# A hybrid decoder layer in fp32: FFN and per-layer gate as Strassen products, the FFN's state in DRAM, the input projection in two kinds of passes, attention dealt out over the passes

## The chip, the core and the metric

The kernel runs on one NeuronCore of a Trainium2 chip. Its five engines run their own instruction streams and wait for each other by semaphores: TensorE (PE; its weight loads are listed apart as PEld), VectorE (DVE), ScalarE (ACT), GpSimd (POOL) and SyncE (SP), which here issues every DMA. The metric is the device time of one execution, in microseconds (us).

## The reference

One layer of a decoder trunk; 2048 tokens, model width 1024, everything fp32.

```python
u = rmsnorm(h, attn_pre_norm); proj = u @ w_in                  # 1024 -> 3584 columns
hq, hf, hi, hg, sq, sk, sv = split(proj)                        # 7 pieces of 512 columns
o_hg = rmsnorm(hgrn2_mix(hq, hf, hi, lb), hg_out_norm) * silu(hg)   # gated recurrence, 4 heads of 128x128 state
o_sb = rmsnorm(stick_breaking_mix(sq, sk, sv), sb_out_norm)         # 8 heads of width 64, strictly causal
h = h + rmsnorm(concat(o_hg, o_sb) @ w_out, attn_post_norm)
u = rmsnorm(h, ffn_pre_norm)
gate, up = split(u @ w_gate_up)                                 # 1024 -> 2 x 2816
y = (silu(gate) * up) @ w_down                                  # 2816 -> 1024
h = h + rmsnorm(y, ffn_post_norm)
out = h + (p @ ple_proj) * sigmoid(h @ ple_gate)                # p: 256 wide; gate 1024 -> 1024
```

Stick-breaking attention weighs key s for query t by sigmoid(z_ts) times the product of (1 - sigmoid(z_tj)) over the keys j between them: a running product along the keys, from the query backwards.

## The kernel before

The 2048 tokens are four groups of 512 (`GT`), g = 0 to 3. Every dense product is made of tiles of 128 x 128 (held in the array) by 128 x 512 (streamed), and each is computed three times for precision: an fp32 operand is split into a high part that the array takes and the remainder (`split`, L185-L189: ACT copies the high part, POOL or DVE subtracts), and `mm3` (L200-L203) adds high x high, high x low and low x high in a PSUM bank. Of a weight tile (`wr` raw, `wh` high, `wl` low; 128 x 512, loaded by SP, four raw buffers) ACT makes `wh` (L187) and POOL makes `wl` (L188). `dense` (L208) takes one weight tile after the other and issues four `mm3`, that is 12 matmuls of 512 columns, for each.

There are 3584 such `mm3`: 896 in the input projection, 256 in the output projection, 1408 in the gate and up half of the FFN, 704 in its down half, 256 in the per-layer gate and 64 in the projection of p.

The order of the work on PE is written out by hand: generators yield in small steps, and `weave` deals the steps of side streams evenly over the slots of a main stream. All other engines get their order from a scheduler that takes each instruction when its inputs should be ready, earlier program text first.

The side streams are attention and HGRN2. An attention unit is 128 queries by up to 512 keys of one head: PE makes `z` (L351), ACT the two sigmoids `f` and `be` (L359, L361), DVE the running product `pt` (a scan, L365) and the weights `a` = be x pt (L367); four units later PE transposes `a` into bank `tr` (L378), ACT and DVE split it into `ah` and `al` (L381, L383), PE multiplies by the values (`av`, L394-L395). There are 320 units: 32, 64, 96 and 128 for the four groups. HGRN2 runs in 45 steps a group: PE products in bank `hg`, masks and products on DVE (`score` L460, `ks` L480, `pd` L482) and on POOL (`qp` L478).

The stages follow each other like this. For each g, all seven pieces of the input projection of g (56 slots), with the attention units whose keys are ready and HGRN2 of g-1 between them. Then for g = 0 output projection and FFN, with the rest of attention (late units of groups 2 and 3) and HGRN2 of group 3 between them, up to the end of the FFN of group 0. Then for g = 1, 2, 3 output projection, per-layer gate of g-1 and FFN of g, with nothing beside them. The FFN of a group keeps its state (u, hidden tiles, y, h) in SBUF: eleven blocks of 256 gate and 256 up columns, the down product behind every second or third of them, then `post_y` (L686 and L542: norm, gain, residual).

## Time and profile before

| | us |
|---|---|
| runs of the kernel before, median of three | 3211.95 (3210.49 to 3213.1) |
| profiled execution, first to last instruction (span) | 3207.7 |
| PE busy in it | 3124.3 (97%) |
| DVE busy | 1774.9 (55%) |
| ACT busy | 1431.9 (45%) |
| POOL busy | 1494.0 (47%) |
| mean granted TensorE clock | 0.994 |

The span is 4.2 us under the median; that lies around the first and the last instruction. A row of a view names line, engine, operation and tiles (out<-in, `wl<-wr,wh`), shape and count. "Busy" of PE counts a matmul from its start to its modelled end, so PE can be shown busy while it loses a little. The views by window give, for a stretch of the span, its length, then busy time and instruction count of PE, PEld, DVE, ACT and POOL, then the granted clock, the busy share of the DMA engines and GB/s.

### The profile page before, as it was taken

Reading aid. Unit: us, or ns where it says so; the run is one execution under the profiler, and the core shown is the slowest. Engines: PE = TensorE matmul, PEld = TensorE weight load, DVE = VectorE, ACT = ScalarE, POOL = GpSimd, SP = SyncE. Lnnn points to the kernel's source line nnn. Section 1 sums busy time; section 2 is a strip of 40 time slices with the busy share of each in tenths; the row PEclk is TensorE's granted clock in tenths of the full one; section 3 lists DMA queues with packets and bytes.
Section 4 is the critical chain, followed back from the end, with each engine's and each line's share of the span. In section 5 each row is a group of like instructions: output and inputs, shape, how many; then the busy total and the mean of one; then the engine's idle time right before and its main releaser. Section 6 shows DMA issues by size and latency. Waiting matters only on the chain.

```text
span 3207.7 us, 44851 instructions
## 1 busy us (share of the span) xinstructions
PE 3124.3 (97%) x15328; PEld 2555.3 (80%) x15328; DVE 1774.9 (55%) x2492; ACT 1431.9 (45%) x2608; POOL 1494.0 (47%) x1254
## 2 busy tenths in 40 slices
PE   8999999999999799999999999999999998999999
PEld 6878878888888678888887888887888887888877
DVE  3356889888888888888866221226222226222142
ACT  4454565555456555555555332334333334332233
POOL 5444434443445423343346444556444556444453
PEclk9999999999999899999999999999999999999999
DMA  7666455545545233333343433332433333333333
GB/s 199 196 178 207 145 173 162 162 144 148 168 138 183 74 93 114 99 113 97 102 134 101 145 96 95 109 112 93 148 98 96 118 106 92 99 94 95 94 107 103
DMA packets 308420, 403.56 MB, mean 126 GB/s; under 512 B 35808, under 2 KB 177120, under 8 KB 308192
## 3 DMA queue, kind: packets, MB, share of 16 engines
q1 hardware_dynamic: 308192, 400.70, 41.1%
q8 instruction: 121, 1.98, 0.3%
q14 instruction: 107, 0.88, 0.1%
HBM read 341.85 MB, written 58.72 MB: 125 GB/s over the span
## 4 chain that ended last, share of the span: by engine, by line
PE 73%; DVE 6%; POOL 3%; issue 2%; ACT 1%; DMA 1%; SPq 0%; DVEq 0%; POOLq 0%; ACTq 0%
PE mm L201 16%; PE mm L203 15%; PE mm L202 15%; PE z L351 3%; PE tr L378 3%; PE av L201 2%; PE z L203 2%; PE z L201 2%; PE av L203 2%; PE av L202 2%; PE z L202 2%; DVE pt L365 2%; PE hg L449 2%; PE av L395 2%; POOL wl L188 1%
## 5 line engine op out<-in xcount | busy, mean ns | idle before, releaser
L188 POOL TENSOR_TENSOR wl<-wr,wh 128x512 fp32r<-128x512 f32 x896 | 1198.7, 1339 | 1415.0 <-ACT wh L187 1239.5
L187 ACT CAST wh<-wr 128x512 fp32r<-128x512 f32 x896 | 555.1, 620 | 1252.4 <-PE mm L202 422.5
L201 PE MATMUL mm<-uh,wh 128*128 128x512 f32 x1696 | 694.5, 410 | 5.3 <-DVE ea L321 4.6
L203 PE MATMUL mm<-uh,wl 128*128 128x512 f32 x1696 | 668.9, 394 | 1.0 <-POOL wl L188 0.9
L202 PE MATMUL mm<-ul,wh 128*128 128x512 f32 x1696 | 665.7, 393 | 0.0
L203 PEld LDWEIGHTS mm<-uh,wl 128*128 128x128 f32 x1696 | 318.6, 188 | 75.6 <-POOL wl L188 2.3
L201 PEld LDWEIGHTS mm<-uh,wh 128*128 128x128 f32 x1696 | 320.2, 189 | 68.9 <-DVE ea L321 5.6
L202 PEld LDWEIGHTS mm<-ul,wh 128*128 128x128 f32 x1696 | 320.3, 189 | 59.8
L365 DVE TENSOR_TENSOR_SCAN pt<-f,cy 128x513 f32<-128x513 f32 x192 | 294.5, 1534 | 69.1 <-ACT f L359 68.1
L645 DVE TENSOR_TENSOR tmp<-mm,tmp 128x512 f32<-128x512 f32 x67 | 45.4, 688 | 428.8 <-ACT tmp L644 428.6
L367 DVE TENSOR_TENSOR a<-be,pt 128x512 f32<-128x512 f32 (+2 forms) x320 | 256.7, 802 | 27.8 <-ACT ah L381 0.5
L381 ACT CAST ah<-tr 128x512 fp32r<-128x512 f32 (+1 forms) x320 | 167.1, 522 | 212.9 <-PE tr L378 209.7
L201 PE MATMUL mm<-wh,uh 128*128 128x512 f32 x616 | 255.0, 414 | 0.3 <-DVE ea L308 0.3
L202 PE MATMUL mm<-wl,uh 128*128 128x512 f32 x616 | 242.3, 393 | 8.0 <-POOL wl L188 8.0
L203 PE MATMUL mm<-wh,ul 128*128 128x512 f32 x616 | 243.0, 394 | 0.0
L365 DVE TENSOR_TENSOR_SCAN pt<-f 128x129 f32<-128x129 f32 (+3 forms) x128 | 163.4, 1277 | 124.6 <-ACT f L359 124.5
L383 DVE TENSOR_TENSOR al<-tr,ah 128x512 fp32r<-128x512 f32 (+1 forms) x320 | 192.4, 601 | 44.1 <-ACT ah L381 43.2
L359 ACT ACTIVATE f<-z 128x512 f32<-128x512 f32 (+2 forms) x320 | 170.0, 531 | 98.9 <-PE z L351 58.9
L201 PE MATMUL mm<-wh,hdh 128*128 128x512 f32 x520 | 209.0, 402 | 0.3 <-DVE tok L664 0.2
L203 PE MATMUL mm<-wh,hdl 128*128 128x512 f32 x520 | 205.3, 395 | 0.0
L202 PE MATMUL mm<-wl,hdh 128*128 128x512 f32 x520 | 205.0, 394 | 0.0
L351 PE MATMUL z<-kt,q 128*128 128x512 f32 (+3 forms) x640 | 183.7, 369 | 0.0
(252 smaller groups left out, 5157.2 us busy)
## 6 DMA issues: line engine op xcount, KB each, us to landing
wr<-in_w_gate_up_dram SPq DMA_DIRECT2D x704, 128.0 KB, 2.2
wr<-in_w_in_dram SPq DMA_DIRECT2D x224, 256.0 KB, 3.0
wr<-in_w_down_dram SPq DMA_DIRECT2D x176, 256.0 KB, 2.6
kt<-k_s SPq DMA_DIRECT2D x80, 256.0 KB, 3.0
vt<-v_s SPq DMA_DIRECT2D x80, 256.0 KB, 3.0
q<-q_s SPq DMA_DIRECT2D x128, 128.0 KB, 3.5
wr<-in_w_out_dram SPq DMA_DIRECT2D x64, 256.0 KB, 2.7
wr<-in_ple_gate_dram SPq DMA_DIRECT2D x64, 256.0 KB, 2.6
```

The lines of the kernel that those rows point to most:

```text
L187: nc.scalar.copy(hi, src)
L188: (lo_engine or nc.gpsimd).tensor_tensor(lo, src, hi.bitcast(F32), op=ALU.subtract)
L201: nc.tensor.matmul(o, l[0], r[0], start=start, stop=False)
L202: nc.tensor.matmul(o, l[0], r[1], start=False, stop=False)
L203: nc.tensor.matmul(o, l[1], r[0], start=False, stop=stop)
L351: nc.tensor.matmul(z[:, :n], st["q"][i][:, tb * P:(tb + 1) * P], ch["k"][:, :n], start=i == 0, stop=i == 1 and not diag)
L359: nc.scalar.activation(f[:, o:GT], z[:, :n], AF.Sigmoid, scale=-0.125)
L365: nc.vector.tensor_tensor_scan(pt[:, o:][:, ::-1], fr, fr, init, op0=ALU.mult, op1=ALU.bypass)
L367: nc.vector.tensor_tensor(a[:, :n], be[:, :n], pt[:, o + 1:], op=ALU.mult)
L378: nc.tensor.transpose(tr[:, tb * P:(tb + 1) * P], ch["a"][tb][:, sb * P:(sb + 1) * P], ident)
L381: nc.scalar.copy(hi[:, lo_c:], tr[:, lo_c:])
L383: nc.vector.tensor_tensor(lo[:, lo_c:], tr[:, lo_c:], hi[:, lo_c:].bitcast(F32), op=ALU.subtract)
```

## The change

**Products.** The gate/up product, the down product and the per-layer gate now work on two groups (1024 tokens) at a time and use one level of Strassen's scheme in Winograd's form: seven half-size block products in place of eight, with sums and differences of blocks before and behind them. The count of `mm3` falls from 1408 to 1232, from 704 to 616 and from 256 to 224; the other 1216 stay. The sums of weight blocks are made for each 256 columns anew on DVE (gate/up, per-layer gate) or POOL (down). The sums of `u` blocks (`t_set`) and of `h` blocks (`s_set`) are made once per pair of groups, those of the hidden tiles on POOL when they are produced. The results are combined by `chain` from PSUM on DVE, the down product keeps 28 tiles `y` and combines them in `post_y`, all on DVE and POOL.

**State in DRAM.** `u`, the residual `h` and `h2`, the transposed `u` and `h2`, the transposed p and seven hidden tiles per block go to DRAM scratch and come back by DMA.

**Prepared steps.** `drive` issues, for step n of a list of stages, first the loads, sums and splits (`prepare`) of step n+3 (gate/up, down) or n+1 (per-layer gate), then PE's products and `chain` of step n (`run`). All raw tiles come from ten `wr` buffers.

**Passes.** The input projection is cut into pass "a" (k, q, v: 24 slots) and pass "b" (the four HGRN2 pieces: 32 slots), in the order a0, a1, b0, a2, b1, a3, b2, b3. `plan` gives each pass its attention units and HGRN2 steps. The rest, 68 units, and HGRN2 of group 3 run with the output projections of groups 0, 1 and half of 2. The output projection of group 3 is put on PE behind the second step of the first gate/up stage. Attention is over when that stage begins.

**`a` on POOL.** The product be x pt moves from DVE to POOL.

```diff
-            nc.vector.tensor_tensor(a[:, :n], be[:, :n], pt[:, o + 1:], op=ALU.mult)
+            nc.gpsimd.tensor_tensor(a[:, :n], be[:, :n], pt[:, o + 1:], op=ALU.mult)
...
+    plan = [
+        ("a", 1, units[0], 0), ("b", 0, units[1] // 2, 0),
+        ("a", 2, units[1] - units[1] // 2, 19), ("b", 1, 44, 26),
+        ("a", 3, 32, 19), ("b", 2, 40, 26), ("b", 3, 40, 38),
+    ]
...
+    rates = Rate(att_stream, 2, todo, 2 * OP_SLOTS + OP_SLOTS // 2)
...
+    def t_set(blk, out, prod):
+        nk = ND // 2
+        if prod in (1, 2):
+            out[prod] = [pair_of(load(blk(prod - 1, 0, k)), "u", prod, G) for k in range(nk)]
+        elif prod == 6:
...
+        elif prod == 3:
+            out[3], out[5], out[4] = [], [], []
+            for k in range(nk):
+                b22, b21 = load(blk(1, 1, k)), load(blk(1, 0, k))
+                out[3].append(pair_of(b22, "u", 3, G))
+                sub(V, b21, b22, b21)
+                b12, b11 = load(blk(0, 1, k)), load(blk(0, 0, k))
+                sub(V, b12, b12, b11)
+                out[5].append(pair_of(b12, "u", 5, V))
+                sub(V, b21, b21, b12)
+                out[4].append(pair_of(b21, "u", 4, G))
...
+    def gate_up(grp):
...
+            def prepare(prod):
...
+                elif prod == 6:
+                    w, a21, a22 = wload(0, 0), wload(1, 0), wload(1, 1)
+                    s["s1"] = [acc("s1") for _ in range(2)]
+                    for n in range(2):
+                        add(V, s["s1"][n], a21[n], a22[n])
+                        sub(V, w[n], s["s1"][n], w[n])
...
+                s[prod] = [pair_of(t, "w", prod, G) for t in w]
+                if fb == 0:
+                    t_set(ublk, tt, prod)
+            def run(prod):
+                for q in range(2):
+                    b = mm_bank()
+                    for k in range(ND // 2):
+                        o = (k % 2) * 256 + q * P
+                        mm3(b, [t[:, o:o + P] for t in s[prod][k // 2]], tt[prod][k], k == 0, k == ND // 2 - 1)
+                    chain(prod, cs[q], b)
...
+    def down(grp):
...
+            def prepare(prod):
+                hs = [pair_in(hid_s[grp][f0 + k, prod - 1], prod, V) for k in range(nk)]
...
+                s[prod] = (hs, [pair_of(t, "w", prod, G) for t in w])
+            def run(prod):
...
+                    else:
+                        add(V, accs[i][prod], b, accs[i][prod])
+                if f0 + nk == nfb and prod == DOWN[-1]:
+                    for i in range(TT):
+                        post_y(grp, i, accs[i])
+    def post_y(grp, i, y):
+        add(G, y[2], y[1], y[2])
...
+        for half, halves in enumerate(((y[2], y[3]), (y[4], y[5]))):
+            r = row_rstd(halves)
+            for j, t in enumerate(halves):
+                gy = load(ffn_post_norm[0:1][:, cs].to_broadcast((P, GT)))
+                nc.vector.scalar_tensor_tensor(t, t, r, gy, op0=ALU.mult, op1=ALU.mult)
+                hr = load(h_s[g][i * P:(i + 1) * P, cs])
+                add(V, t, t, hr)
+                nc.sync.dma_start(h2_s[g][i * P:(i + 1) * P, cs], t)
+    def drive(stages, hooks):
+        steps = [(a, st, i, n) for a, (st, n) in enumerate(stages) for i in range(len(st))]
+        done = 0
+        for at, (a, st, i, n) in enumerate(steps):
+            while done < len(steps) and done <= at + steps[done][3]:
+                _, st2, i2, _ = steps[done]
+                st2[i2][0]()
+                done += 1
+            st[i][1]()
...
+    stages = [(gate_up(0), 3), (down(0), 3), (gate_up(1), 3), (down(1), 3), (ple(0), 1), (ple(1), 1)]
+    stages[0][0][2] = (lambda: (start_last(), third[0]()), third[1])
```

Three places show how the order moves.

POOL beside the output projection with attention. Before, beside the FFN of group 0 with attention and HGRN2 of group 3 (`qp` is HGRN2's, `wl` the split of a weight tile):

```order
L478 TENSOR_TENSOR qp<-qp,pd 128x64x4
L188 TENSOR_TENSOR wl<-wr,wh 128x512 x3
L478 TENSOR_TENSOR qp<-qp,pd 128x32x8
L188 TENSOR_TENSOR wl<-wr,wh 128x512 x3
L478 TENSOR_TENSOR qp<-qp,pd 128x16x16
```

Now (output projection of group 1), where `a` is the attention weight of a unit:

```order
L388 TENSOR_TENSOR a<-be,pt 128x512
L499 TENSOR_TENSOR qp<-qp,pd 128x32x8
L207 TENSOR_TENSOR wl<-wr,wh 128x512
L388 TENSOR_TENSOR a<-be,pt 128x512
L499 TENSOR_TENSOR qp<-qp,pd 128x16x16
L388 TENSOR_TENSOR a<-be,pt 128x512
L207 TENSOR_TENSOR wl<-wr,wh 128x512
L388 TENSOR_TENSOR a<-be,pt 128x512
```

Between two weight splits there stand now one or two `a`, which wait for DVE's scan.

DVE at the end of the down product. Before, `post_y` of a group is twelve instructions (four of them 1024 wide), and behind it come the splits of the transposed tiles and the next output projection:

```order
L666 TENSOR_TENSOR tok<-mm,tok 128x512 x3
L542 SCALAR_TENSOR_TENSOR tok<-tok,rstd_22280,tmp 128x512 x2
L542 SCALAR_TENSOR_TENSOR tok<-tok,rstd_22287,tmp 128x512 x2
L686 TENSOR_TENSOR h<-h,tok 128x1024 x2
L542 SCALAR_TENSOR_TENSOR tok<-tok,rstd_22294,tmp 128x512 x2
L686 TENSOR_TENSOR h<-h,tok 128x1024
```

Now, behind the first down stage, the tail of `post_y` stands ahead of the last sums of `u` blocks (`wr<-wr`), which the fourth step of the second gate/up stage needs:

```order
L954 SCALAR_TENSOR_TENSOR y<-y,rstd_24161,wr 128x512
L725 TENSOR_TENSOR y<-y,wr 128x512
L954 SCALAR_TENSOR_TENSOR y<-y,rstd_24184,wr 128x512
L725 TENSOR_TENSOR y<-y,wr 128x512
L954 SCALAR_TENSOR_TENSOR y<-y,rstd_24184,wr 128x512
L725 TENSOR_TENSOR y<-y,wr 128x512
L722 TENSOR_TENSOR wr<-wr 128x512 x5
L709 TENSOR_TENSOR ul<-wr,uh 128x512
L722 TENSOR_TENSOR wr<-wr 128x512 x3
L709 TENSOR_TENSOR ul<-wr,uh 128x512
```

From the last result of the down product to the first two of these sums there are 61 DVE instructions.

DVE where a per-layer gate begins. Before (group 0), it takes the gate's results from PSUM, adds the residual, and splits the next group's transposed tiles:

```order
L714 TENSOR_TENSOR tok<-mm,tok 128x512
L715 TENSOR_TENSOR tok<-tok,h 128x512
L714 TENSOR_TENSOR tok<-mm,tok 128x512
L714 TENSOR_TENSOR tok<-z,tok 128x512
L715 TENSOR_TENSOR tok<-tok,h 128x512
L251 SCALAR_TENSOR_TENSOR ul<-tr,g_ffn,uh 128x512
```

Now the splits of the second step (`ul<-wr,uh` x4) stand behind all of `post_y`, and the sums and splits of the third step behind those:

```order
L725 TENSOR_TENSOR y<-y,wr 128x512
L709 TENSOR_TENSOR ul<-wr,uh 128x512 x4
L725 TENSOR_TENSOR wr<-wr 128x512
L725 TENSOR_TENSOR c_30873<-tr,cu 128x512
L722 TENSOR_TENSOR wr<-wr 128x512 x3
L725 TENSOR_TENSOR wr<-wr 128x512
L709 TENSOR_TENSOR ul<-wr,uh 128x512
L725 TENSOR_TENSOR c_30888<-mm,cu 128x512
```

The last result of the down product stands 46 instructions ahead of the end of those four splits, and the last split of the third step 35 further on.

748 lines of the change are left out of this document (488 added, 260 removed).

## The prediction

> **What bounds the kernel now.** I read the page's busy times and its chain first, then windows, then the rows of the instructions that the change multiplies.
>
> ```profile
> span 3207.7 us, 44851 instructions
> PE 3124.3 (97%) x15328; PEld 2555.3 (80%) x15328; DVE 1774.9 (55%) x2492; ACT 1431.9 (45%) x2608; POOL 1494.0 (47%) x1254
> PE 73%; DVE 6%; POOL 3%; issue 2%; ACT 1%; DMA 1%; SPq 0%; DVEq 0%; POOLq 0%; ACTq 0%
> ```
>
> PE is busy for 3124 of 3208 us and carries the chain: the kernel is PE-bound, and 83 us are all the idle time that a better order alone could win. The windows (length, then busy time and count of PE, PEld, DVE, ACT, POOL, then clock, DMA share, GB/s) show where the 83 lie and what a matmul costs:
>
> ```profile
> 0.00:80.00 80.00, 65.86 (x290) 53.34 (x291) 24.50 (x44) 34.85 (x60) 40.57 (x61) 1.00 0.71 199
> 480.00:560.00 80.00, 77.22 (x449) 64.18 (x448) 72.69 (x112) 42.17 (x83) 32.68 (x29) 1.00 0.60 164
> 1080.00:1120.00 40.00, 23.11 (x107) 17.19 (x108) 38.24 (x65) 22.34 (x43) 20.09 (x22) 0.70 0.13 37
> 1680.00:1760.00 80.00, 74.32 (x342) 59.19 (x340) 53.30 (x58) 42.16 (x74) 55.40 (x50) 1.00 0.34 107
> 1840.00:1920.00 80.00, 80.00 (x345) 64.39 (x344) 18.26 (x26) 24.69 (x41) 36.93 (x29) 1.00 0.31 93
> 2160.00:2240.00 80.00, 77.19 (x359) 62.42 (x358) 48.62 (x55) 36.54 (x63) 50.26 (x46) 1.00 0.30 95
> 2640.00:2720.00 80.00, 74.01 (x344) 59.45 (x342) 50.00 (x54) 38.52 (x67) 52.74 (x49) 1.00 0.30 93
> ```
>
> From 1840 to 1920 PE does nothing but FFN products: 345 matmuls in 80 us, 0.232 us each, with DVE busy for 18 and POOL for 37 us. From 480 to 560, with attention beside the input projection, DVE is busy for 72.7 of 80. At 1080 to 1120 PE stands for 17 us at clock 0.70: the chain there runs through the norm between output projection and FFN of group 0.
>
> ```profile
> 1091.40 5.39 POOL rstd L224
> 1099.33 1.21 DVE h L614
> ```
>
> **What is removed on PE.** The products fall from 3584 to 3288 `mm3`: 296 x 3 = 888 matmuls fewer, transposes unchanged. 888 x 0.232 = 206 us. PE's busy time becomes 3124 - 206 = 2918 us. This is counted; the question is what the other engines give back.
>
> Old idle time that goes with the old stage boundaries: 17 us at 1080 to 1120 (the output projections of groups 1 and 2 now stand between this norm and its reader), 6 at 1680, 3 at 2160 and 6 at 2640: together 32, and some 3 us of the slow clock, so 35. The 14 us of the start stay.
>
> **What is added on DVE and POOL.** Rows of single instructions, ns min/median/max, and mean behind the bar:
>
> ```profile
> L365 DVE TENSOR_TENSOR_SCAN pt<-f,cy x192: 1265/1299/2409, 336.3 to 1644.7; 128x513 f32<-128x513 f32 x192
> L367 DVE TENSOR_TENSOR a<-be,pt x320: 279/692/1821, 100.2 to 1646.1; 128x512 f32<-128x512 f32 x96, 128x128 f32<-128x128 f32 x32, 128x384 f32<-128x384 f32 x32
> L188 POOL TENSOR_TENSOR wl<-wr,wh x896: 1260/1292/2463, 17.4 to 3193.8; 128x512 fp32r<-128x512 f32 x180
> L188 DVE TENSOR_TENSOR hdl<-tmp,hdh x88: 669/679/1794, 1176.5 to 3080.5; 128x512 fp32r<-128x512 f32 x88
> L542 DVE SCALAR_TENSOR_TENSOR tok<-tok,rstd,tmp x64: 716/747/1784, 1082.0 to 3122.9; 128x512 f32<-128x512 f32 x64
> L383 DVE TENSOR_TENSOR al<-tr,ah 128x512 fp32r<-128x512 f32 x224 | 152.7, 682 | 30.1 <-ACT ah L381 29.3
> L478 POOL TENSOR_TENSOR qp<-qp,pd 128x256 f32<-128x256 f32 x112 | 96.9, 865 | 185.8 <-PE hg L449 102.0 <-issue 33.0 <-PE hg L456 17.2
> L480 DVE TENSOR_TENSOR ks<-ks,pd 128x256 f32<-128x256 f32 x112 | 62.4, 557 | 2.2 <-PE hg L456 2.1
> ```
>
> A 512-wide step is 1.26 to 1.29 us on POOL and 0.67 to 0.69 on DVE. But DVE instructions whose inputs are both in SBUF (L365, L367, L188, L542) reach 1.8 to 2.4 us, while `al`, which reads PSUM, has a mean of 682 ns, as good as its best. The timeline shows why, in three pairs (start us, us):
>
> ```profile
> 405.03 1.93 DVE L365 TENSOR_TENSOR_SCAN pt<-f 128x513 f32<-128x513 f32 x1 [1.98 <-ACT f L359]
> 404.58 1.29 POOL L188 TENSOR_TENSOR wl<-wr,wh 128x512 fp32r<-128x512 f32 x1 [3.67 <-ACT wh L187]
> 338.03 1.82 DVE L367 TENSOR_TENSOR a<-be,pt 128x512 f32<-128x512 f32 x1
> 338.01 1.29 POOL L188 TENSOR_TENSOR wl<-wr,wh 128x512 fp32r<-128x512 f32 x1 [1.17 <-ACT wh L187]
> 378.73 1.26 DVE L365 TENSOR_TENSOR_SCAN pt<-f,cy 128x513 f32<-128x513 f32 x1
> 379.07 2.02 POOL L188 TENSOR_TENSOR wl<-wr,wh 128x512 fp32r<-128x512 f32 x1 [1.06 <-ACT wh L187]
> ```
>
> They take turns. The scan ends 1.09 us after POOL's end (405.87), DVE's product 0.55 after it (339.30), and in the last pair POOL ends 1.10 after the scan (379.99). So a turn costs 1.09 us for a scan, 0.55 for a DVE step, 1.10 for a POOL step: about 0.2 us of each lie under the other's turn. I go by the trace's turns.
>
> The Trainium skill has a rule for this in "SBUF — State Buffer", section "SBUF: two separate sides": the port pair that DVE and POOL share is an exclusive lock, kept for the whole instruction. The trace agrees on exclusive, not on whole (1.09 against 1.27 us); by the rule the turns of the stretch below would be 1385 us in place of 1103.
>
> The stretch of attention (pass a1 to the first half of output projection 2). PE: 248 weight tiles x 12 x 0.232 = 690 us, and attention, HGRN2 and transposes: 3124 - 10,752 x 0.232 = 630 at most, of which some 75 lie elsewhere: 1245. Turns: POOL 248 splits, 272 whole-tile worths of `a` (the change moves it from 0.55 on DVE to 1.10 here) and 52 others, 572 x 1.10 = 629; 112 `qp` at 0.55 = 62; small ones 43; DVE 272 scans x 1.09 = 296, HGRN2, norms and residuals 73. Sum 1103, 89% of PE's time. By passes the share is 72 to 90% up to b3, but 100 to 115% in the output projections, where 68 units and 52 HGRN2 steps meet 40 slots: 299 us of turns against 275 of PE. DVE's own work there is 241 us before it waits for any turn. So at least 299 - 275 = 24 us; in-order engines do not fill every turn: I take 35 there (0 if turns overlap more, 85 at 83% filled) and 15 in the passes (0 to 45).
>
> **The FFN stretch.** A gate/up block of seven steps is 7 x 24 x 0.232 = 39 us of PE; turns: 18 POOL steps x 1.10 + 16 DVE x 0.55 = 29; DVE in all 16 x 0.68 + 14 x 0.68 = 20. A down block has the same 39 us; turns 22 x 1.10 + 14 x 0.55 = 32, DVE 14 x 0.68 + 28 x 0.68 = 29. Both fit under PE; 15 for the places where they do not (0 to 40).
>
> ```profile
> q1 hardware_dynamic: 308192, 400.70, 41.1%
> 20.00:25.00 5.00, 5.00 (x23) 4.12 (x23) 3.38 (x5) 2.44 (x6) 1.16 (x1) 1.00 0.90 300
> wr<-in_w_down_dram SPq DMA_DIRECT2D x176, 256.0 KB, 2.6
> ```
>
> DMA: the list of issues gives 623 MB in place of 401. At the 300 GB/s seen at a share of 0.90 a tile of 256 KB takes 0.87 us; a down block loads 30 tiles, 26 of 39 us; it fits. The state's way through DRAM lies behind prepared steps of 5.6 us, three ahead, against 2.6 us to landing.
>
> What is late is the joints, where `post_y` (52 DVE steps, 48 tiles of DMA) meets the next stage's first sums. Down to gate/up 1: the fourth step waits for 61 DVE instructions, 61 x 0.68 = 42 us, up to 58 at the mean of about 0.95 that such rows reach beside POOL; ACT and POOL add 2; three steps of PE, 17 us, cover: 27 to 43, I take 35 (10 if the last block hides more, 55 if its DMA, 66 tiles, is late too). Down to per-layer gate: 46 instructions, 31 to 44 us, less one step of 11: 22 to 35, I take 28; the third step 35 more, 24 to 33 less 11: 17. In the second per-layer gate, behind 22 us of projection, 8. The two projections of p move 40 tiles, 35 us, against 22 of PE, partly ahead of time: 6 each. Per-layer gates together 65 (30 to 110). Start of the first gate/up stage: 48 loads, 42 us, under 25 + 11 + 45 us of output projections and two steps: 10 (0 to 30). Slow clock after such waits, by the 0.70 above: 8 (0 to 20).
>
> **Sum.** 3208 - 206 - 35 + 35 + 15 + 15 + 35 + 65 + 10 + 8 = 3150 us.
>
> **Rivals.** *The harvest comes in whole:* every new term at its lower end, 40 us: 3208 - 241 + 40 = 3007. For it: DVE busy for 72.7 of 80 us hardly cost PE anything before. Against it: the joints are counted in instructions that stand in line. *Turns cost the whole instruction* (1.29 us on POOL, 1.27 a scan, 0.67 a DVE step): the attention stretch then needs 885 us of POOL and 500 of DVE, 1385 against PE's 1245, +140; joints and gates at their contended prices 43 and 90, the rest 40: 3208 - 241 + 313 = 3280, slower. It decides from 241 us of new idle time on, and queues that leave one turn in five unused come to the same. For it: the 2.4 us that scans reach, and a POOL that goes from 1494 us busy to some 2100. Against it: the 0.2 us of overlap in each pair. It is what the rule of the Trainium skill above would give. *The steps are not prepared:* ten `wr` buffers hold four tiles for three steps in the down product, so loads come late and each of its 84 steps waits about 0.8 us: 3150 + 65 = 3215, no change. Against it: 30 tiles of 2.6 us in 39 us need two buffers at a time.
>
> **Chances.** Forecast 0.50 (own range 3085 to 3215), whole harvest 0.17, whole turns 0.27, unprepared steps 0.06. The range must reach into both sides: 3050 to 3270. A measurement tells about 0.2%, 6 us, from no change: faster 0.66 (harvest and nearly all of the forecast), same 0.07, slower 0.27.
>
> **What would show it.** Right: PE busy 2900 to 2950; windows of pure gate/up still 345 matmuls per 80 us; waits of PE of 20 to 45 us behind the first down stage, twice in the first per-layer gate; PE at 85 to 92% in the output projections with DVE above 90%; POOL busy near 2100. Wrong: PE idle spread over the down stages (loads), idle above 150 us in the attention stretch (turns), or no joint above 10 us (harvest).

## The result: 8% slower

| | before | after |
|---|---|---|
| median of the runs, us | 3211.47 (3210.49 to 3213.1) | 3470.64 (3469.27 to 3471.91) |
| ratio to before, 95% interval | | 1.0809 (1.0794 to 1.0824) |
| profiled execution, span, us | 3207.7 | 3470.1 |
| mean granted clock | 0.994 | 0.934 |

The forecast was 3150 (3050 to 3270): wrong in sign and outside the range. The page of the changed kernel:

```profile
span 3470.1 us, 46357 instructions
PE 3016.4 (87%) x14440; PEld 2451.2 (71%) x14440; DVE 2285.9 (66%) x3130; ACT 1542.4 (44%) x2963; POOL 2089.8 (60%) x1780
PEclk9999999999999998788898899998799998997889
```

PE has its 888 matmuls fewer (15328 to 14440), and its idle time went from 83 to 454 us. The clock row, full everywhere before but at one place, drops in many places from about 1300 us on.

To see where, I split PE's time by its products in program order (line L222 ends each `mm3`). *Pure work* is the count of each form of PE instruction times its median spacing in the same run; *loss* is the length less that. From PE's first to its last end, before has 3083 of pure work and 110 of loss, after 2826 and 624. So the harvest on PE is 257 us and the loss 514 more.

| stretch of after, us | length | pure work | loss |
|---|---|---|---|
| pass a0 (14 to 95) | 81 | 72 | 8 |
| passes a1 to b3, with attention (95 to 1161) | 1066 | 955 | 110 |
| output projections 0, 1 and half of 2, with attention (1161 to 1549) | 389 | 249 | 140 |
| rest of projection 2, projection 3, two gate/up steps (to 1655) | 105 | 81 | 25 |
| gate/up 0 (to 2148) | 494 | 419 | 75 |
| down 0 (to 2389) | 241 | 210 | 31 |
| gate/up 1 (to 2911) | 522 | 427 | 95 |
| down 1 (to 3144) | 233 | 210 | 23 |
| gates and projections of p (to 3465) | 321 | 203 | 118 |

One place runs in another order than the change was described: projection 3 is issued with the preparation of the third gate/up step, and `drive` asks for that ahead of the first step's products. In the trace projection 3 runs from 1580 to 1643 us, and the first two gate/up steps come behind it.

The windows show the character of these stretches (length, busy time and count of PE, PEld, DVE, ACT, POOL, clock, DMA share, GB/s):

```profile
820.00:930.00 110.00, 109.88 (x632) 91.72 (x631) 85.61 (x123) 63.45 (x123) 73.50 (x67) 1.00 0.47 144
1161.00:1549.00 388.00, 291.77 (x1573) 236.24 (x1572) 260.33 (x386) 192.85 (x390) 223.02 (x224) 0.88 0.39 123
1433.00:1474.00 41.00, 12.71 (x45) 9.61 (x44) 25.65 (x42) 13.52 (x36) 20.36 (x31) 0.59 0.52 178
1700.00:1780.00 80.00, 80.00 (x355) 66.24 (x354) 50.44 (x69) 24.76 (x42) 51.80 (x37) 1.00 0.56 176
1824.00:1844.00 20.00, 11.42 (x46) 8.84 (x45) 8.02 (x6) 6.64 (x12) 10.72 (x8) 0.74 0.83 275
2154.00:2178.00 24.00, 10.70 (x26) 6.74 (x25) 23.17 (x19) 10.07 (x19) 20.68 (x13) 0.57 0.52 178
2389.00:2476.00 87.00, 35.93 (x102) 23.75 (x101) 74.80 (x96) 29.00 (x62) 48.45 (x43) 0.61 0.73 248
3144.00:3243.00 99.00, 42.50 (x147) 30.75 (x147) 75.03 (x108) 36.11 (x74) 40.22 (x42) 0.67 0.71 244
```

Where nothing special happens PE is full: inside a pass with attention beside it (820 to 930), and in gate/up (1700 to 1780), at 355 matmuls in 80 us. The loss is not spread; it stands at events. In the FFN that is plain to see when each step's length is taken from the ends of its last matmul. A step of eight `mm3` is 5.4 us; of the 222 full-size steps behind the first two in the two gate/up and two down stages all but 25 are 5.4 to 5.6. The longest, with the gates' (10.9 us of pure work):

| step | us | what is there |
|---|---|---|
| gate/up 0, step 4 | 28.2 | sums of `u`, norm behind projection 3 |
| gate/up 0, blocks 5 to 8, second step | 19.1, 18.3, 15.8, 20.3 | transposes of `u` (L641) behind the first step |
| gate/up 1, same places | 13.7, 17.3, 13.2, 15.2 | transposes of `h2` |
| down 0 and 1, second step | 23.5, 25.2 | end of gate/up |
| gate/up 1, steps 3 and 4 | 27.0, 47.7 | `post_y` of down 0 |
| first gate, steps 2 and 3 | 51.4, 36.0 | `post_y` of down 1 |
| second gate, step 3 | 36.0 | sums of `h` |

### The profile page after: what moved, and what is told of

Its sections match the earlier page's. It is cut to its first block, busy times and chain, and to the rows that moved or that the text cites. A ratio compares the mean times of both kernels' runs of the same rounds, so it can differ in the third digit from the quotient of the medians.

```text
span 3470.1 us, 46357 instructions
## 1 busy us (share of the span) xinstructions
PE 3016.4 (87%) x14440; PEld 2451.2 (71%) x14440; DVE 2285.9 (66%) x3130; ACT 1542.4 (44%) x2963; POOL 2089.8 (60%) x1780
## 5 line engine op out<-in xcount | busy, mean ns | idle before, releaser
L220 PE MATMUL mm<-uh,wh 128*128 128x512 f32 x1344 | 555.7, 413 | 50.1 <-ACT uh L708 37.0
L222 PE MATMUL mm<-uh,wl 128*128 128x512 f32 x1344 | 532.7, 396 | 1.1 <-POOL wl L709 1.0
L388 POOL TENSOR_TENSOR a<-be,pt 128x512 f32<-128x512 f32 (+2 forms) x320 | 315.3, 985 | 351.7 <-DVE pt L386 290.6
L220 PE MATMUL mm<-wh,uh 128*128 128x512 f32 x1008 | 427.0, 424 | 65.7 <-ACT y L929 16.1
L221 PE MATMUL mm<-wl,uh 128*128 128x512 f32 x1008 | 408.2, 405 | 5.1 <-POOL wl L709 5.1
L222 PE MATMUL mm<-wh,ul 128*128 128x512 f32 x1008 | 407.8, 405 | 0.0
L222 PEld LDWEIGHTS mm<-uh,wl 128*128 128x128 f32 x1344 | 256.5, 191 | 58.3 <-POOL wl L709 1.8
L220 PEld LDWEIGHTS mm<-wh,uh 128*128 128x128 f32 x1008 | 197.8, 196 | 112.5 <-ACT y L929 18.9
L718 DVE TENSOR_TENSOR ul<-ul,uh 128x512 fp32r<-128x512 f32 x154 | 163.7, 1078 | 119.5 <-ACT uh L717 113.0
L221 PEld LDWEIGHTS mm<-wl,uh 128*128 128x128 f32 x1008 | 198.0, 196 | 43.5 <-POOL wl L709 9.0
L222 PEld LDWEIGHTS mm<-wh,ul 128*128 128x128 f32 x1008 | 197.2, 196 | 44.0
```

The lines of the kernel that those rows point to most:

```text
L220: nc.tensor.matmul(o, l[0], r[0], start=start, stop=False)
L221: nc.tensor.matmul(o, l[0], r[1], start=False, stop=False)
L222: nc.tensor.matmul(o, l[1], r[0], start=False, stop=stop)
L388: nc.gpsimd.tensor_tensor(a[:, :n], be[:, :n], pt[:, o + 1:], op=ALU.mult)
```

## Experiments

Losses are read by the same stretches and steps in every run. Ratios are to the kernel before, on the same chip.

### The transposes between steps

The waits of PE in the first gate/up stage (line waited < releaser: us, times, longest):

```profile
PE hg L641 <- ACT acc L647: 30.4, 12, 7.0
PE mm L220 <- ACT uh L708: 9.3, 2, 5.4
```

Four blocks of transposes stand behind one step and share the one bank `hg`. The timeline of PE (start, us, engine, line, instruction, idle before it and its releaser) at one place:

```profile
1832.46 1.12 PE L641 MATMUL hg<-ident,wr 128*128 128x128 f32 x4 [7.03 <-ACT acc L647]
1834.36 1.12 PE L641 MATMUL hg<-ident,wr 128*128 128x128 f32 x4 [0.78 <-ACT acc L647]
1836.25 1.11 PE L641 MATMUL hg<-ident,wr 128*128 128x128 f32 x4 [0.78 <-ACT acc L647]
```

```diff
-                b = bank(tag)
+                b = mm_bank() if tag is None else bank(tag)
...
-        st = Stream(turn(src, dst, gain, "hg", new_wr, acc))
+        st = Stream(turn(src, dst, gain, None, new_wr, acc))
```

> The changed kernel with one edit: the transposes of u and h2 between FFN and gate steps (four blocks behind one step) take their PSUM banks from the ring of seven that the products use, in place of the one bank they shared. Theory 'one bank': PE waits because block n+1 needs the bank that ScalarE empties only after what stands ahead in its queue. Then the eight steps behind such a place, now 13 to 20 us long in place of 5.4, become 5.4 plus 1.9 us of transposes, 7.3: about 45 us less in the first gate/up stage, 30 in the second, 10 to 15 in the first per-layer gate; 3470 - 85 = 3385 us. Rival 'ScalarE is late anyway': its queue waits for GpSimd's splits, so the products behind the transposes would stand for the same banks; the eight steps stay above 12 us and the time above 3450.

Measured: **3386.39 us**, 1.0549 (1.0531 to 1.0566). The eight steps are 7.2 us, one of them 8.8; the first gate/up stage loses 33 (before this edit 75), the second 64 (95), the first gate 74 (85). PE's waits for L647 are gone. The transposes themselves, by line, in the changed kernel and in this run (ns min/median/max):

```profile
L641 PE MATMUL hg<-ident,wr x64: 270/421/477, 1824.8 to 1988.1; 128*128 128x128 f32 x64
```

```profile
L641 PE MATMUL mm<-ident,wr x32: 270/272/273, 1824.1 to 1944.7; 128*128 128x128 f32 x32
```

The other 32 stand in the banks `z`, `av` and `tr`, at the same 272. Without the wait the clock stays up (1.00 in this run's window from 1815 to 1835 us, where the changed kernel has 0.74 from 1824 to 1844), and a transpose takes 272 ns in place of 421. "One bank" is shown, with 84 us.

### `a` on GpSimd, and turns

```diff
-            nc.gpsimd.tensor_tensor(a[:, :n], be[:, :n], pt[:, o + 1:], op=ALU.mult)
+            nc.vector.tensor_tensor(a[:, :n], be[:, :n], pt[:, o + 1:], op=ALU.mult)
```

> The changed kernel with the attention weight a = be x pt back on VectorE. Theory 'turns': in the attention stretch VectorE and GpSimd exclude each other; a costs 1.10 us of turn on GpSimd and 0.55 on VectorE, so 272 whole tiles free 150 us of turns. PE's lost time in the output projections that stand beside attention (about 140 us over its pure work) falls to 60 or less, in the passes (about 110) to 80 or less: 3470 - 110 = 3360 us. Rival 'VectorE's own queue': it is busy 70 to 77% there and late in order, not by turns; 218 us more of work on it make the stretch longer by 30 to 80 us: 3500 to 3550. If PE's waits there come from elsewhere, within 15 us of 3470.

Measured: **3526.94 us**, 1.0983 (1.0962 to 1.1003), 56 us slower than the changed kernel. PE's waits from the passes to the end of attention, first in the changed kernel, then here:

```profile
PE av L416 <- DVE al L404: 26.7, 26, 4.3
PE tr L641 <- DMA xt<-un_s: 25.8, 4, 17.2
PE hg L470 <- DVE ks L501: 14.1, 4, 7.6
PE mm L220 <- DVE vv L321: 12.9, 9, 5.0
```

```profile
PE av L416 <- DVE al L404: 59.0, 53, 5.8
PE hg L470 <- DVE ks L501: 22.0, 7, 8.4
```

Fewer turns, more waits: PE's waits for VectorE grow, and the time falls into the range of "VectorE's own queue". The opposite edit, `a` left out (`be` takes over its eight buffers, where it had two):

```diff
-            nc.gpsimd.tensor_tensor(a[:, :n], be[:, :n], pt[:, o + 1:], op=ALU.mult)
-            ch["a"].append(a)
+            ch["a"].append(be)
```

> The changed kernel, with the product a = be x pt left out of the computation: PE transposes be in its place. 320 GpSimd instructions go, some 300 us of turns, and VectorE's own work stays as it is. Theory 'turns': VectorE's scans no longer wait for a, its busy time in the attention stretch (95 to 1549 us: about 900) falls by 100 or more, and what PE loses there over its pure work (about 250) falls to 150: 3470 - 100 = 3370 us. Rival 'VectorE's own work and order': VectorE stays 60 to 75% busy with the same instructions in the same order, and PE's loss stays above 215: 3440 or more.

Measured: **3426.82 us**, 1.0677 (1.0656 to 1.0698), 44 us less. VectorE's busy time falls by 64 us in the whole kernel, not by 100 in the stretch, and the loss from 250 to 212, just under the rival's line. So turns, with `a`'s own latency, are worth about a sixth of the loss beside attention. And the move alone, on the kernel before:

```diff
-            nc.vector.tensor_tensor(a[:, :n], be[:, :n], pt[:, o + 1:], op=ALU.mult)
+            nc.gpsimd.tensor_tensor(a[:, :n], be[:, :n], pt[:, o + 1:], op=ALU.mult)
```

> The kernel before, with one edit taken from the change: a = be x pt on GpSimd. Theory 'turns': GpSimd's turns grow by 150 us net between 80 and 1660 us, its splits and VectorE's scans come later, and the time grows by 10 to 40 us: 3235. Rival 'VectorE's own queue': 218 us of work leave VectorE there, PE's waits for it (41 us in all) halve, and the time falls by 10 to 25 us: 3195. By the second, the move was the change's gain and something else in the stretch its loss.

Measured: **3187.56 us**, 0.9930 (0.9914 to 0.9947): 0.7% under the kernel before, small but clear of the noise. Windows of the kernel before, then of this run:

```profile
80.00:1040.00 960.00, 942.55 (x5277) 783.69 (x5276) 732.65 (x1087) 516.53 (x1016) 429.67 (x367) 1.00 0.56 167
1120.00:1660.00 540.00, 532.35 (x2756) 435.79 (x2756) 452.75 (x628) 294.56 (x548) 194.53 (x155) 1.00 0.34 102
```

```profile
80.00:1040.00 960.00, 950.00 (x5337) 795.15 (x5336) 649.97 (x913) 521.97 (x1028) 604.62 (x559) 1.00 0.57 168
1120.00:1660.00 540.00, 539.89 (x2769) 445.81 (x2769) 366.35 (x505) 295.55 (x549) 313.10 (x274) 1.00 0.36 108
```

VectorE gives 169 us away, GpSimd takes 294 on, and PE's idle time beside attention falls from 25 to 10 us of 1500. Beside attention the one-line move is a gain; the loss there comes from the rest of the change.

### Beside the output projections

The 140 us between 1161 and 1549 have no single owner. Four runs, each taking one thing away. First the transposes of group 0 (`t0`) go to the second half of projection 2, beside those of group 1 (`t1`):

```diff
-            tu = Stream(turn(un_s[0], u_s[0], g_ffn, "tr", xt, ev))
-            weave(op, n, rates.part(n), r3.part(n, 1), (tu, ND, 0))
+            weave(op, n, rates.part(n), r3.part(n, 1))
...
-            tu = Stream(turn(un_s[1], u_s[1], g_ffn, "tr", xt, ev))
-            weave(op, n, (tu, ND, 0))
+            t0 = Stream(turn(un_s[0], u_s[0], g_ffn, "tr", xt, ev))
+            t1 = Stream(turn(un_s[1], u_s[1], g_ffn, "av", xt, ev))
+            weave(op, n, (t0, ND, 0), (t1, ND, 1))
```

> The changed kernel with the transposes of u of group 0 moved from the first half of the third output projection, where attention ends, to its second half, beside those of group 1. Theory 'PE stands for their loads': the tiles they load into are held by the norm behind the second output projection, and PE, in order, waits 25.8 us for the loads and 12.8 for the shared bank; the first half (116 us for 52 of pure work) loses 35, the second half gains 5 to 8: 3470 - 30 = 3440 us. Rival 'attention's end': the last 30 units and the recurrence are late by themselves, the half stays above 105 us and the time above 3460.

Measured: **3449.63 us**, 1.0749 (1.0728 to 1.0770), 21 us less; the first half of projection 2 loses 34 (before 64), the second 10 (6). PE stood for the transposes' loads: these waits fall from 25.8 to 5.2 us. Then HGRN2 of group 3 is left out, here and in the two calls behind:

```diff
-            weave(op, OP_SLOTS - 6, rates.part(OP_SLOTS - 6), r3.part(OP_SLOTS - 6, 1))
+            weave(op, OP_SLOTS - 6, rates.part(OP_SLOTS - 6))
```

> The changed kernel, with HGRN2 of group 3 left out of the computation beside the output projections (the projection of group 3 takes group 2's result). Attention runs there as before, in the same slots. HGRN2's own work on PE is about 20 us. Theory 'round trips of HGRN2': each of its 45 steps goes from PE to VectorE and GpSimd and back, in 34 slots, and PE stands in order; then PE's loss in the output projections beside attention (140 us over its pure work) falls to 70 or less: 3470 - 20 - 70 = 3380 us. Rival 'the attention units themselves': the loss stays above 110: 3430 to 3450.

Measured: **3413.44 us**, 1.0635 (1.0614 to 1.0657). HGRN2's own work was 38 us, not 20 (pure work 249 to 211), and the loss falls only to 116: its round trips are worth 24 us.

```diff
-        chunks = [(g, h, c) for g in range(NG) for h in range(SBH) for c in range(g, -1, -1)]
+        chunks = [(g, h, c) for g in range(NG) for h in range(SBH if g < 3 else 4) for c in range(g, -1, -1)]
```

> The changed kernel, with attention heads 4 to 7 of group 3 left out of the computation (the projection of group 3 takes group 2's results there): beside the output projections 4 attention units are left of 68, HGRN2 of group 3 stays. The 64 units' own work on PE is 87 us. Theory 'density of attention': PE's loss there (140 us over pure work) falls to 50: 3470 - 87 - 90 = 3293 us. Rival 'the projections' own turnover' (four banks to be emptied every four slots, norms, the wait for the transposes' loads): it stays above 95: 3340 or more.

Measured: **3340.85 us**, 1.0409 (1.0388 to 1.0430). The loss falls to 85: 55 us belong to attention, and 85 stand with hardly any: 4.6, 7.4 and 28.4 of them in the first slots of the three projections (6.8, 14.2 and 34.0 in the changed kernel).

```diff
-            for part in range(2):
-                for banks in dense(HH, src, ops[part * HH:(part + 1) * HH], False):
+            for banks in dense(2 * HH, src, ops, False):
```

> The changed kernel with the output projection accumulated over all eight row blocks at once in place of two parts of four; its four banks are then emptied every eight slots in place of every four. Both emptying instructions stay, so ScalarE and VectorE do the same work; the separate scaling of the two halves is left out of the computation. Theory 'turnover of banks': PE's loss beside the output projections lies in the first one or two slots behind each emptying (6.8, 2.3, 9.0, 3.0, 9.7 and 3.4 us behind those that go); the loss of 140 us there falls to 110 or less: 3438 us. Rival 'turns and density': the loss only moves to other slots and stays above 130: 3462 or more.

Measured: **3484.71 us**, 1.0861 (1.0839 to 1.0883). The loss behind the emptying that goes does vanish (6.8 to 0.1 us in the fifth of 16 slots of projection 0), and comes back at the one that stays (ninth slot 1.4 to 7.4); the stretch still loses 132 and the next half 19 in place of 6. The first slot of each of the three projections, behind the norm of the one before, keeps 6.5, 15 and 37 us. Turnover is refuted as the owner. The shares found (55 attention, 24 HGRN2, about 26 the transposes, about 25 `a`) overlap, so they don't make a sum.

### The joints

The tails first: norm and residual (`post_y`), and the last hidden block's gating, sums and stores, are put behind the next preparation.

```diff
-                    for i in range(TT):
-                        post_y(grp, i, accs[i])
+                    later.append(lambda: [post_y(grp, i, accs[i]) for i in range(TT)])
...
                 done += 1
+            while later:
+                later.pop(0)()
             st[i][1]()
```

> The changed kernel with the tails of stages put behind the next step's preparation in the program: the norm and residual behind a down stage, and the gating, sums and stores of the last hidden block behind a gate/up stage. Nothing is added or left out. Theory 'the next stage's preparation stands behind the tail': the second steps of the down stages (23.5 and 25.2 us in place of 5.4) fall below 10, together 30 us less; the third and fourth steps of the second gate/up stage (27.0 and 47.7) lose 25 us together, since three steps' worth of banks cover part of the tail; the second step of the first per-layer gate (51.4 in place of 10.9) loses 20 to 30: 3470 - 80 = 3390 us. Rival 'VectorE's work itself': the joint after a down stage holds about 100 VectorE instructions, 75 us, whatever their order; waits move from one step to the next and only the 30 us of the down stages come back: 3440.

Measured: **3479.73 us**, 1.0841 (1.0825 to 1.0858): no gain. The second steps of the down stages stay at 24.0 and 25.0. In gate/up 1 steps 3 to 5 are 27.3, 20.0, 37.3 in place of 27.0, 47.7, 6.3; in the gate steps 2 and 3 are 10.9 and 68.4 in place of 51.4 and 36.0. The wait only moves on, as the rival had it. Then less work and fewer loads:

```diff
-                nc.vector.scalar_tensor_tensor(t, t, r, gy, op0=ALU.mult, op1=ALU.mult)
-                add(V, t, t, hr)
+                nc.vector.scalar_tensor_tensor(t, t, r, hr, op0=ALU.mult, op1=ALU.add)
```

> The changed kernel, with the gain of the norm behind the down product left out of the computation: the scaling by the row's rstd is taken into the residual addition, 16 VectorE instructions fewer at each of the two joints behind a down stage. The gain's 16 tiles are still loaded. Theory 'VectorE's work at the joint': at 0.78 us each (74.8 us for 96 instructions there) the first five steps of the second gate/up stage (92.8 us together) and the first three steps of the first per-layer gate (98.8) lose 12 us each, whichever step shows it: 3470 - 25 = 3445 us. Rival 'the joint's loads and stores' (248 GB/s there): both stay within 3 us, and so does the time.

Measured: **3461.65 us**, 1.0786 (1.0764 to 1.0807). The first five steps of gate/up 1 fall from 92.8 to 89.2, the first three of the gate from 98.8 to 90.8: 4 and 8, between the theory's 12 each and the rival's 3.

```diff
+        if i == 0:
+            gains[:] = [y[1], y[6]]
+            for j in range(2):
+                nc.sync.dma_start(gains[j], ffn_post_norm[0:1][:, j * GT:(j + 1) * GT].to_broadcast((P, GT)))
...
-                gy = load(ffn_post_norm[0:1][:, cs].to_broadcast((P, GT)))
-                nc.vector.scalar_tensor_tensor(t, t, r, gy, op0=ALU.mult, op1=ALU.mult)
+                nc.vector.scalar_tensor_tensor(t, t, r, gains[j], op0=ALU.mult, op1=ALU.mult)
```

> The changed kernel with the gain of the norm behind the down product loaded once for each joint (two tiles) in place of 16 times. All arithmetic stays. Theory 'DMA at the joint': in the second half of the norm, VectorE's pairs come every 1.95 us and wait 0.5 us each for a load; three tiles of 256 KB move in that time, 403 GB/s. With two tiles a pair takes VectorE's own 1.44 us, and the first five steps of the second gate/up stage (92.8 us) and the first three of the first per-layer gate (98.8) lose 8 to 12 us each: 3470 - 20 = 3450 us. Rival 'VectorE's instructions alone': each loses under 3 us, 3465 or more.

Measured: **3462.29 us**, 1.0792 (1.0774 to 1.0810): 3 and 4 us, just above the rival's line. Neither the instructions nor the loads alone set the joint. The timelines of the changed kernel suggest why: three limits follow each other. First GpSimd, where the split that PE waits for stands behind a norm's sum. The sum waits 8.65 us for ScalarE, and is then itself shown for 6.98 us. Rows of GpSimd, then VectorE, then PE:

```profile
2399.80 6.98 POOL L251 TENSOR_TENSOR ssum<-ss 128x1 f32<-128x1 f32 x1 [8.65 <-ACT junk L249]
...
2407.67 1.26 POOL L709 TENSOR_TENSOR wl<-wr,wh 128x512 fp32r<-128x512 f32 x1
```

```profile
2405.45 1.29 DVE L725 TENSOR_TENSOR y<-y 128x512 f32<-128x512 f32 x2
2407.74 1.74 DVE L954 SCALAR_TENSOR_TENSOR y<-y,rstd,wr 128x512 f32<-128x512 f32 x1 [1.00 <-POOL rstd L243]
```

```profile
2408.98 0.79 PE L222 MATMUL tr<-uh,wl 128*128 128x512 f32 x1 [7.83 <-POOL wl L709]
...
2451.46 0.79 PE L220 MATMUL mm<-uh,wh 128*128 128x512 f32 x1 [23.77 <-ACT uh L708]
```

The same instruction (L251) takes 275 ns in the median of its 64 occurrences. Over these 6.98 us VectorE works through twelve instructions without a gap; its last one ends at 2406.74 and the sum at 2406.78. So GpSimd seems to have been shut out until VectorE's row ended; no run tested that. Then the loads, with 0.5 us of wait in each pair of `post_y`, 1.95 us apart; then turns, one round of sums and splits for step 4 in 4.55 us (VectorE, then GpSimd):

```profile
2446.18 0.69 DVE L725 TENSOR_TENSOR y<-y,wr 128x512 f32<-128x512 f32 x1 [0.51 <-DMA wr<-h_s]
...
2448.15 0.69 DVE L725 TENSOR_TENSOR y<-y,wr 128x512 f32<-128x512 f32 x1 [0.56 <-DMA wr<-h_s]
...
2456.71 4.03 DVE L722 TENSOR_TENSOR wr<-wr 128x512 f32<-128x512 f32 x3
2460.66 0.68 DVE L709 TENSOR_TENSOR ul<-wr,uh 128x512 fp32r<-128x512 f32 x1
2461.26 4.03 DVE L722 TENSOR_TENSOR wr<-wr 128x512 f32<-128x512 f32 x3
```

```profile
2461.47 3.27 POOL L709 TENSOR_TENSOR ul<-wr,uh 128x512 fp32r<-128x512 f32 x2 [1.28 <-ACT uh L708]
```

This order of limits is read from the trace; no run took all three away. For the other joint, gate/up to down, the trace offered a chain: PE waits for ScalarE's copy of `y`, behind a split, behind a load, behind a store on SyncE that waits for VectorE. ScalarE's wait in it, from 2148 to 2178:

```profile
ACT uh L717 <- DMA ul<-hid_s: 12.4, 4, 10.2
```

```diff
-                        nc.sync.dma_start(hid_s[grp][fb, i - 1], t)
+                        (nc.gpsimd if fb == DFF // 256 - 1 else nc.sync).dma_start(hid_s[grp][fb, i - 1], t)
```

> The changed kernel, with the 14 stores of the last hidden block of each gate/up stage issued by GpSimd in place of SyncE. Theory 'a chain over four queues': behind the second step of a down stage PE waits for ScalarE's copy of y, which stands behind a split, which waits 10.2 us for a hidden tile's load, which stands on SyncE behind a store that waits for VectorE's gating. With the store elsewhere the load comes 5 to 10 us earlier and the second steps (23.5 and 25.2 us) fall to 14: 3470 - 20 = 3450 us. Rival 'VectorE and GpSimd take turns there' (VectorE busy for 31 of 36 us, its splits at 1.75 in place of 0.69): the steps stay above 20 and the time within 5 us, or grows by GpSimd's issuing.

Measured: **3478.23 us**, 1.0836 (1.0818 to 1.0854). In down 0 the second and third steps are 18.5 and 11.9 in place of 23.5 and 6.0, in down 1 26.3 and 12.8 in place of 25.2 and 8.1. So the place of the stores on SyncE does not set it. Loads are not ruled out, since ScalarE waits for hidden tiles as long as before (from 2148 to 2184, 13.4 us in all for 13.3; the longest 4.5 for 10.2). In the second step of down 0 of the changed kernel, PE itself waits 7.2 us for VectorE's emptying of banks (`cu`, L722) and 6.1 for ScalarE's copy, and VectorE was busy for 23.17 of the 24 us in the window above. The rival is the likelier, but it was not tested by itself.

### The gate as plain products

```diff
-        steps = [(lambda p=prod: prepare(p), lambda p=prod: run(p)) for prod in CHAIN]
+        steps = [(lambda a=a: prepare(*a), lambda a=a: run(*a))
+                 for a in [(h, j, i) for h in range(2) for j in range(2) for i in range(2)]]
```

> The changed kernel with one part undone: the per-layer gate as plain products again, 256 mm3 in place of 224 (22 us more on PE), in eight steps of four weight tiles for two groups; no sums of h or of weights, 32 splits of h in place of 56, no combining on VectorE. Theory 'the gate's sums and splits': they stand on VectorE beside the norm behind the down stage, and PE loses 118 us over its pure work in the two gates and projections of p; without them the loss falls to 50 or less: 3470 + 22 - 68 = 3424 us. Rival 'norm and loads alone': the loss stays above 100 and the time goes to 3480 or more.

Measured: **3436.29 us**, 1.0710 (1.0694 to 1.0726); the loss in the two gates and projections of p falls from 118 to 59. First and second gate:

```profile
3150.80:3303.60 152.80, 105.28 (x450) 83.95 (x450) 50.30 (x71) 57.94 (x111) 62.23 (x60) 0.83 0.66 221
3325.40:3413.30 87.90, 87.62 (x385) 71.92 (x384) 18.09 (x25) 36.50 (x63) 41.38 (x32) 1.00 0.60 197
```

The second gate loses nothing any more, the first still 40 us in its second step (51.3), behind `post_y`, and some 18 in the four steps that have transposes in them. Strassen on the gate cost 34 us more than it won.

### Together

Transposes in the ring (not in the gate), transposes of group 0 later, the gate plain, and one edit more:

```diff
-                if fb == 0:
+                if fb == 0 and prod in (1, 2):
                     t_set(ublk, tt, prod)
+                elif fb == 0 and prod == 6:
+                    t_set(ublk, tt, 6)
+                    t_set(ublk, tt, 3)
```

> The changed kernel with four edits together: transposes between FFN steps in the products' ring of banks; those of u of group 0 in the second half of the third output projection; the sums and splits of the fourth gate/up step's u made with the third's; the per-layer gate plain. If the losses are separate: 75 + 21 from the first two as measured, 45 by the estimate for the plain gate, and about 15 at the start of the first gate/up stage (its fourth step takes 28 us in place of 5.4): 3470 - 156 = 3315 us. If they hide one another on VectorE's queue: 3350 or more. In either case above the kernel before, since what PE loses beside attention (about 230 us) stays.

Measured: **3356.15 us**, 1.0456 (1.0441 to 1.0472). That is in the range of "they hide one another", but the earlier sums are a part of it: they gained nothing, step 4 of gate/up 0 is 32.5 (28.2 before this edit), of gate/up 1 53.2 (47.7). With the gain loaded once in their place:

> The changed kernel with four edits together: transposes between FFN steps in the products' ring of banks (84 us by itself), those of u of group 0 later (21), the per-layer gate plain (34), the gain loaded once (20 expected). If they add up: 3470 - 159 = 3311 us. The four edits of the run before gave 114 in place of 139 for the same first three, with an earlier u step that gained nothing in its place: if they hide one another: 3335 to 3350.

Measured: **3338.03 us**, 1.0406 (1.0390 to 1.0423), 133 us less than the changed kernel. By the stretches these edits touch, the single runs give 72 (transposes, in the two gate/up stages only, as here) + 21 + 34 + 8 = 135: these losses are separate. The time lies in the range that the forecast gave for losses that hide one another, since its sum took 84 for the transposes, the gate's included, and 20 for the gain. It is still 4% above the kernel before; `a` on GpSimd in the kernel before is the best version found.

## Why the prediction was wrong, point by point

| step of the forecast | forecast, us | found, us |
|---|---|---|
| products on PE | -206 | -257 |
| attention stretch, over what before loses there (59 without its old joint) | +50 | +191 |
| start of the first gate/up stage | +10 | +48 |
| gate/up and down, steady | +15 | 137: transposes 75, gate/up to down 41, small ones 21 |
| joint down 0 to gate/up 1 | +35 | +64 |
| per-layer gates | +65 | +118, some 12 of it transposes |
| slow clock | +8 | inside the above |

The differences make 317 of the 320 us between forecast and result (7 us of old loss in the FFN are gone, and the clock's 8 are not counted twice).

- **Products.** Counted rightly, 888 fewer. The harvest is larger since the FFN's products now stand 0.225 us apart (355 in 80 us) where they were 0.232.
- **"Transposes unchanged."** This step was right as a count and failed as a price: I costed them at nothing and named no cover. Before, they lay in the streams between products; now four blocks in a row share one bank. 84 us, shown by the ring of banks.
- **The attention stretch.** The term was worked out from turns ("I take 35 there and 15 in the passes") and is the largest miss. Turns were the wrong measure: inside a pass PE is 99.9% busy with VectorE at 78%, `a` back on VectorE made it worse by 56 us, and leaving `a` out gave 44. In the passes about 30 of the 110 us stand in their first slots and 27 beside the transposes of the next `u`; beside the projections the loss has several owners. My count of 299 us of turns against 275 of PE looked for a full engine, and none is full: VectorE is busy for 67% there, not above 90% as I wrote. What I put at nothing is the boundaries: of the 140 us beside the projections 55 stand in their first slots (34 of these where PE stands mostly for the transposes' loads), and 85 are left with hardly any attention beside them. Which queue owns the rest stays open.
- **The FFN stretch.** "Both fit under PE" holds: nearly every step is 5.4 us, the 30 tiles per down block too. The failure is at its edges: I named the joint behind a down stage and passed over the one from gate/up to down.
- **Start of the first gate/up stage.** I priced it by its loads under 81 us of cover, and both were wrong. Some 19 of the 48 us are lost in projection 3, 12.1 of them in one wait behind its first four slots, for a bank that ScalarE empties (`mix`, L601). Another 23 are lost in step 4. Its preparation stands behind projection 3 in the program, so only three steps of 5.4 us cover it. PE waits for no load there, but 9.3 us for ScalarE's `uh` and 8.9 for GpSimd's `ul`, and the sums ahead of both stand in VectorE's row among projection 3's norm (L621) and residual (L622); VectorE is busy for 22.56 of the 23 us from 1660 to 1683:

```profile
1660.95 2.73 DVE L621 SCALAR_TENSOR_TENSOR mix<-mix,rstd,gb 128x512 f32<-128x512 f32 x4
1663.60 1.28 DVE L722 TENSOR_TENSOR wr<-wr 128x512 f32<-128x512 f32 x2
...
1667.40 1.15 DVE L622 TENSOR_TENSOR h<-h,mix 128x512 f32<-128x512 f32 x1
1668.47 1.75 DVE L722 TENSOR_TENSOR wr<-wr 128x512 f32<-128x512 f32 x1
```

  The earlier sums, made with the third step's preparation, stayed behind projection 3 too, and gained nothing.
- **Joint down 0 to gate/up 1.** The place was right, the size not: 64, above my upper bound of 55. The fourth step lost 42, inside my 27 to 43; the third, which I had not named, lost 22. The line of 61 VectorE instructions took 59 us (2389.4 to 2448.8), near the 58 of my upper price. What I had too small is what comes behind it: rounds of 4.55 us for the sums and splits, where I had 2 us for ScalarE and GpSimd. And the early wait for GpSimd I did not have at all.
- **Gates.** Places right, both steps of the first, sizes too small: 40 and 25 us for 28 and 17. The second gate's third step lost 25, where I had 8 in all. With plain products the third steps lose nothing and the second step of the first gate keeps its 40: the sums and splits own the third steps, and what makes the second long is `post_y`'s joint.
- **Clock.** About 113 us of after's loss (32 before) are instructions that follow each other without a wait but more than 5% above their median spacing; 90 of these (11 before) stand where the granted clock is below full. I had priced the clock from one stall of before.
- **What would show it.** Right: POOL busy 2090 for "near 2100", DMA 623 MB, waits of 23.8 us behind the first down stage and 36.9 in the first gate. Wrong: the second wait there, 14.2 us for 20 to 45; 355 matmuls per 80 us of gate/up for 345; PE busy 3016 for 2900 to 2950, since a matmul at half clock counts longer (nine in 3 us, below), and PE at 75% in the projections for 85 to 92. My sign "idle above 150 us in the attention stretch (turns)" came true, about 158, and would have named the wrong cause.
- **Rivals.** The time lies beyond all three. "Turns cost the whole instruction" had the sign, by the wrong mechanism: the rounds at the joint take 4.55 us, near the 4.40 of two splits at 1.10 and four VectorE steps at 0.55, where whole instructions would take 5.26. By the Trainium skill's page "SBUF — State Buffer", section "SBUF: two separate sides", the lock is held for the whole instruction; the trace agrees that it excludes, not on that length. Nor are turns always taken in alternation: at the joint one GpSimd sum was shown for 6.98 us, over twelve VectorE instructions.

## What to carry to other kernels

Price a reorganisation by its events, not by shares of busy time: list every place where PE's own stream holds something other than the steady product (a transpose, a joint, the first slot of a stage), and name for each the bank, the queue ahead of its releaser and the cover. Fewer products on PE are worth their full count only while the steady state is the whole; here it ran without a gap, and what stands between gave back twice the gain. And when a change has several parts, time the cheap one alone: one moved instruction was worth 0.7% by itself, and the rest of the change without it cost 9.8%.

## What the runs showed of the hardware

- **Half clock after a stop.** Behind the transposes' stop the windows of the changed kernel show the granted clock at 0.51 and nine products in 3 us, then 45 in 10 at 1.00:

```profile
1837.00:1840.00 3.00, 3.00 (x9) 2.42 (x8) 0.00 (x0) 0.69 (x1) 0.00 (x0) 0.51 1.06 400
1840.00:1850.00 10.00, 10.00 (x45) 8.24 (x45) 3.17 (x5) 3.02 (x5) 3.79 (x3) 1.00 0.40 137
```

  The Trainium skill's page "TensorE: Matmul & The Clock Gate", section "Part 1: The HAM clock gate (the "warmup" mystery)", gives half rate after an idle window of about 3.4 us. The trace agrees: the stop ahead was 7.03 us.
- **GpSimd beside a VectorE that never pauses.** A GpSimd sum of 128x1 values that takes 275 ns in the median took 6.98 us and ended with VectorE's row of instructions. In all seven GpSimd instructions over 2.6 us in the changed kernel (up to 4.84 us for a split with a median of 1.30) VectorE ran without a gap, five to twelve instructions long; the kernel before has such a place in `rstd` at 1091.40, 5.39 us. That one caused the other is likely, not tested.
- **Transposes and the clock.** In the first gate/up stage of the changed kernel the 48 transposes at half the granted clock took 421 ns in the median, the 16 at full clock 272.
- **Matmul spacing.** The same 512-column matmul stands 0.225 to 0.227 us apart in the new FFN and 0.232 in most of the old one. What makes the difference was not tested.
